# Modulation columns at fixed places, low parts of weights divided anew, a first norm that starts with TensorE, tiles 96 bytes further

## The chip, the cores and the metric

One core of a Trainium2 chip runs the whole program in one launch. The metric is the device time of that launch in microseconds (us). TensorE (PE in the profile) multiplies, VectorE (DVE) and ScalarE (ACT) work elementwise, GpSimd (POOL) does small elementwise work and issues some DMAs, and SyncE (SP) issues nearly all the others.

## The reference

A trunk of two layers over 512 frames of 1024 features, float32. Each layer has a token mixer and a SwiGLU network (MLP), both behind an RMS norm that a conditioning vector `c` scales and shifts:

```
mod = silu(c) @ ada_w[l] + ada_b[l]                     # 6 x 1024 columns: shift, scale, gate, twice
h   = rms_norm(x, norm1_g) * (1 + sc1) + sh1
p   = h @ w_in                                          # shifted features, pooled features, gates
ps  = token_shift(p[..., :N_SHIFT])                     # r, k, v, and three small "lora" inputs
y_a = rwkv7_time_mix(ps, ...)                           # a recurrence over the frames, 8 heads of 64
y_b = multiscale_pool(p[..., pooled part])
mixed = gate0 * (y_a @ proj_a) + gate1 * (y_b @ proj_b)
x   = x + gt1 * (mixed @ w_out)
h2  = rms_norm(x, norm2_g) * (1 + sc2) + sh2
x   = x + gt2 * ((silu(h2 @ w_gate) * (h2 @ w_up)) @ w_down)
...
return rms_norm(x, final_g)
```

## The kernel before

**Layout of the work.** Everything is transposed: a tile holds 128 features by 512 frames. A product of float32 accuracy is made of three fast passes: a weight tile `raw` of 128 x 1024 is split into a rounded high part `whi` and the rest `wlo`, the features likewise into `hh` and `hl`, and `block` (L224) issues `whi*hh`, `whi*hl`, `wlo*hh`. A stretch of such passes is called a block here; eight of them make one output tile.

**Low parts.** `weights` (L180) always lets ScalarE round `raw` into `whi`. The low part is made in one of two ways, chosen by `self.by_dma`: VectorE subtracts (`wlo<-raw,whi`, L201), or ScalarE writes `-whi` and a DMA on POOL's queue reads the weight a second time and adds it (L198 and L199). `by_dma = 2` alternates.

**Modulation.** One column of `mod` is a 128 x 1024 row block of `ada` multiplied by the broadcast `silu(c)` (`cact`) and summed, one VectorE instruction (L264, shown as CUSTOM_DVE_ANT_0) and a short read of its sum. `some` (L266) fetches the next row block and multiplies the one fetched before; `self.land` names the buffers for it (spare tiles `ar`, `hf`, `row`), else it lands in a `raw` buffer. There are 96 columns. Sixteen are made in the head, columns 16 to 47 of layer 0 in the first mixer, and the 48 of layer 1 in the first MLP and the second mixer. Where an instruction is not marked to keep its place (`self.exact`, L236), the scheduler chooses where it stands on its engine.

**Stages.** The head (`head`, L294) loads `c` (broadcast to 128 partitions) and `x`, sums squares (`ssum`), forms the reciprocal root (`rstd`, L403) by way of TensorE, and multiplies the first seven groups of columns of `w_in`, whose inputs `nh`, `hh`, `hl` become ready feature group by feature group (k = 0 to 7); for k below 3 the raw weights are used in plain float32. Then for each layer: `loras` and `pooled` (small products and running means), a loop over four head pairs j in which `front` and `back` prepare the recurrence on VectorE, ScalarE and POOL while `SLOT` says how many blocks of the next products run and where `some` is called; `solve` (a triangular inverse, 62 short VectorE instructions in a chain) with 51 blocks of gate products beside it; `chain`, the recurrence over eight chunks, in which TensorE's order is fixed (`pinned`): per chunk the products `z`, `u`, `hp`, `y`, with 1, 2 and 1 blocks of gate products between them (`CHAIN`); the read-out (`read`) with its copies `yn`, `yal`; `proj_a`; `w_out`; the second norm; and the MLP (`mlp`, L1351), in which 22 groups of hidden features, 19 of them by a scheme of seven products (`seven`), are followed by `w_down`.

In one chunk of the recurrence VectorE must deliver, in this order, `zs` (from `z`, needed by `u`), `vt` (from `u`, needed by `hp` and `y`), `hn` and the next `vt` (needed by the next `z`).

## Time and profile before

| | |
|---|---|
| median of 3 runs | 1476.82 us (1475.88 to 1486.47) |
| the profiled execution | 1479.65 us |
| its span, first to last instruction | 1477.9 us |
| mean granted TensorE clock | 0.995 |
| busy: PE, DVE, ACT, POOL | 97%, 74%, 51%, 17% |
| HBM read, written | 269.84 MB, 27.79 MB |

By time from the span's start: head 0 to 62 us, first mixer to 420, first MLP to 757, second mixer to 1125, second MLP and the end to 1478. A row of the timeline gives start, duration, engine, line, operation, output and inputs, and in brackets how long the engine was idle before it and what ended the wait. A row of waits gives the waiting engine and line, what it waited for, the total in us, how often, and the longest. A row of the windows gives, for a stretch of time, each engine's busy time with its count of instructions, the granted clock (1.00 is full), the DMA engines' busy share and GB/s.

### The profile page before, as it was taken

The page shows a single profiled execution, that of the slowest core. Times are in us where ns is not written, and L with a number is a line of the kernel's source. Part 1 is how long each engine was busy: PE and PEld are TensorE (multiplying, and loading weights), DVE is VectorE, ACT ScalarE, POOL GpSimd, SP SyncE. Part 2 cuts the span into 40 slices and gives each one's busy share as a digit, 9 for nine tenths or more (in the row PEclk, how much of TensorE's full clock was granted, in tenths as well). Part 3 has the DMA queues.
Part 4 walks back from the last instruction along what each step waited for, and adds up shares of the span by engine and source line. Part 5 has one row for each costly group of instructions (what it writes and reads, how often), then busy time and mean ns, then how long its engine had stood idle before and what let it go on. Part 6 is the DMA issues. An engine that isn't in the chain of part 4 may idle for free. (4 is left out here: it accounts for less than half of the span.)

```text
span 1477.9 us, 25375 instructions
## 1 busy us (share of the span) xinstructions
PE 1429.7 (97%) x9982; PEld 1219.6 (83%) x9982; DVE 1087.3 (74%) x1846; ACT 751.0 (51%) x1031; POOL 246.8 (17%) x291
## 2 busy tenths in 40 slices
PE   5999998999999999999999999999999999999998
PEld 2767676777899999988897777877789999998887
DVE  7888958576788888876767685768578888887333
ACT  5576544344456656642336766443444656656221
POOL 0133321110022211100012334111102222110000
PEclk9999999999999999999999999999999999999999
DMA  8788689589839999778726747976974899885232
GB/s 319 235 268 238 193 227 254 148 261 271 236 101 230 234 215 226 179 251 287 260 87 180 181 113 168 261 176 191 289 235 131 208 219 223 192 187 169 87 100 71
DMA packets 112918, 299.28 MB, mean 203 GB/s; under 512 B 12128, under 2 KB 22624, under 8 KB 112800
## 3 DMA queue, kind: packets, MB, share of 16 engines
q1 hardware_dynamic: 90160, 227.93, 47.3%
q0 software_dynamic: 21776, 68.69, 25.5%
q8 instruction: 78, 1.28, 0.4%
q10 hardware_dynamic: 864, 1.05, 0.2%
q14 instruction: 40, 0.33, 0.1%
HBM read 269.84 MB, written 27.79 MB: 201 GB/s over the span
## 5 line engine op out<-in xcount | busy, mean ns | idle before, releaser
L221 PE MATMUL acc<-hh,whi 128*128 128x512 f32 (+1 forms) x1119 | 392.5, 357 | 0.2
L221 PE MATMUL acc<-hh,wlo 128*128 128x512 f32 (+1 forms) x1111 | 379.2, 346 | 8.3 <-DMA wlo<-in_w_in 7.5
L221 PE MATMUL acc<-hl,whi 128*128 128x512 f32 (+2 forms) x1119 | 369.3, 346 | 0.1
L195 ACT CAST whi<-raw 128x1024 fp32r<-128x1024 f32 x143 | 149.8, 1049 | 266.8 <-PE acc L221 175.2
L221 PEld LDWEIGHTS acc<-hh,wlo 128*128 128x128 f32 x1111 | 210.7, 190 | 36.7 <-DMA wlo<-in_w_in 9.2
L221 PEld LDWEIGHTS acc<-hh,whi 128*128 128x128 f32 x1119 | 212.1, 190 | 31.9 <-issue 2.4
L221 PEld LDWEIGHTS acc<-hl,whi 128*128 128x128 f32 (+1 forms) x1119 | 203.8, 189 | 26.4 <-issue 2.2
L201 DVE TENSOR_TENSOR wlo<-raw,whi 128x1024 fp32r<-128x1024 f32 x78 | 94.7, 1221 | 77.3 <-ACT whi L195 72.9
L221 PE MATMUL acc<-f,whi 128*128 128x512 f32 (+1 forms) x304 | 92.2, 386 | 0.0
L221 PE MATMUL m<-tl,f13h 128*128 128x256 f32 x304 | 86.0, 283 | 0.0
L221 PE MATMUL m<-th,f13l 128*128 128x256 f32 x304 | 86.0, 283 | 0.0
L221 PE MATMUL m<-th,f13h 128*128 128x256 f32 x304 | 85.9, 283 | 0.0
L241 ACT CAST f24h<-x 128x1024 fp32r<-128x1024 f32 x38 | 39.9, 1050 | 60.4 <-DVE x L241 60.4
L198 ACT ACTIVATE wlo<-raw 128x1024 fp32r<-128x1024 f32 x65 | 68.5, 1053 | 0.1
L221 PEld LDWEIGHTS acc<-f,whi 128*128 128x128 f32 x304 | 56.2, 188 | 12.3
L199 POOL DMA_DIRECT2D wlo<-in_w_in x41 | 35.9, 876 | 159.3 <-ACT wlo L198 159.3
L1283 POOL DMA_DIRECT2D f22l<-in_w_gu x38 | 32.8, 863 | 171.6 <-ACT f22l L241 164.4
L221 PE MATMUL acc<-f,wlo 128*128 128x512 f32 (+1 forms) x152 | 58.7, 386 | 0.0
L241 DVE TENSOR_TENSOR f24l<-x,f24h 128x1024 fp32r<-128x1024 f32 x38 | 46.5, 1224 | 16.3 <-ACT f24h L241 16.3
L221 PEld LDWEIGHTS m<-th,f13h 128*128 128x128 f32 x304 | 58.4, 192 | 0.0
L221 PEld LDWEIGHTS m<-th,f13l 128*128 128x128 f32 x304 | 58.4, 192 | 0.0
L221 PEld LDWEIGHTS m<-tl,f13h 128*128 128x128 f32 x304 | 58.2, 192 | 0.0
(338 smaller groups left out, 3434.0 us busy)
## 6 DMA issues: line engine op xcount, KB each, us to landing
raw<-in_w_in SPq DMA_DIRECT2D x63, 512.0 KB, 4.7
raw<-in_w_gu SPq DMA_DIRECT2D x50, 512.0 KB, 4.5
raw<-in_w_down SPq DMA_DIRECT2D x44, 512.0 KB, 3.5
wlo<-in_w_in POOLq DMA_DIRECT2D x41, 512.0 KB, 7.7
wlo<-in_w_gu POOLq DMA_DIRECT2D x40, 512.0 KB, 6.8
x<-in_w_gu SPq DMA_DIRECT2D x76, 256.0 KB, 4.4
row<-in_ada SPq DMA_DIRECT2D x30, 512.0 KB, 5.2
raw<-in_ada SPq DMA_DIRECT2D x25, 512.0 KB, 4.9
```

Source lines behind the costliest of these rows:

```text
L195: self.on(nc.scalar, "copy")(hi, raw)
L198: nc.scalar.activation(lo, raw, AF.Copy, scale=-1.0)
L199: nc.gpsimd.dma_start(lo, src, accum_op=ALU.add)
L201: self.on(nc.vector, "tensor_tensor")(lo, raw, hi.bitcast(F32), ALU.subtract)
L221: i = (tensor.transpose if transpose else tensor.matmul)(*args, **k).ins
L241: return (lambda *a, **k: self.tc.keep_in_program_order(op(*a, **k))) if self.exact else op
L1283: nc.gpsimd.dma_start(lo, two[:, b], accum_op=ALU.add)
```

## The change

- **Head.** `c` comes as one row of 4 KB instead of a broadcast of 512 KB; two products with a row of ones spread it to 128 partitions, and ScalarE applies silu out of PSUM. TensorE runs 12, 14, 5 and 5 products of ones by ones (`idle`), whose results nobody reads, ahead of and between the steps of the norm. The first two modulation columns are made at fixed places, two of the four scalings `dg` go to ScalarE, and the squares have four buffers instead of two.
- **Columns.** None among the pooled groups (`SOME` 0 instead of 1), three instead of four per head pair at other places, five left for `w_out`, and in the first mixer one each at steps 2, 8, 14 and 20 of the recurrence (`LATER`), all of these marked to keep their place. Columns 40 to 47 of layer 0 move into the first MLP, where twelve instead of eight of its groups make one.
- **Low parts.** `by_dma` alternates for j = 0 and 4 in the first mixer and for j = 2, 3, 4 in the second, where it alternated for 2 and 3; from the end of the recurrence VectorE subtracts them all. In the whole program 112 low parts are subtracted on VectorE instead of 84, 28 fewer by DMA.
- **Order of blocks.** In the second mixer nine instead of three blocks of r, k, v run ahead of `loras`, with two weights loaded ahead, `loras` lands its inputs in halves in other buffers, and gate blocks follow when r, k, v are through.
- **Layout.** A pad of 88 float32 ahead of the left pools and one of 120 at the right edge. In the built program before, the starting addresses of the tiles that TensorE reads are 96, 160 or 224 past a multiple of 256 bytes (a few 64), and of the pairs of a moving tile and the next weights about half differ by 128, 64 or 192 modulo 256 in the 512-wide products; with the pads nearly all start at a multiple of 256, and all but some 70 pairs differ by 0.

```diff
+PADS = (88, 120)
-SOME = 1
+SOME = 0
+
+LATER = (2, 8, 14, 20)
+WARM = (12, 14, 5)
-FIRST = (8, 3)
+FIRST = (8, 9)
-        (0, False, 0), (3, True, 0), (3, False, 1), (2, False, 0), (4, True, 1), (3, False, 0), (3, False, 1),
-        (4, True, 1), (1, False, 0), (1, False, 0),
+        (0, False, 0), (3, True, 0), (3, False, 1), (2, False, 0), (4, True, 0), (3, False, 0), (3, False, 0),
+        (4, True, 1), (1, False, 0), (1, False, 1),
...
+        self.const.tile([P, PADS[0]], F32, name="pad")
+        pool(name="edge", bufs=1, side="right").tile([P, PADS[1]], F32, name="edge")
...
-        nc.sync.dma_start(self.cact, a["c"].partition_broadcast(P))
+        c = w0.tile([1, D], F32, name="c", bufs=1)
...
+        self.pinned = True
+        ps = [self.m() for _ in range(3)]
+        idle = lambda n: [self.mm(ps[2][:, 0:P], self.ones, self.ones, start=True, stop=True) for _ in range(n)]
+        idle(WARM[0])
+
+        def spread(i):
+            cs = slice(i * S, i * S + S)
+            self.mm(ps[i], self.ones[0:1, :], c[:, cs], start=True, stop=True)
+            nc.scalar.activation(self.cact[:, cs], ps[i], AF.Silu)
...
+            if k in (4, 5):
+                spread(k - 4)
+        idle(WARM[1])
         self.soon(AF.Sqrt)
+        self.exact = True
+        self.modulation(0, (KC,), raws)
         self.new_h()
-        rb = self.rstd(ALL)
+        rb = self.rstd(ALL, lambda: idle(WARM[2]))
+        idle(WARM[2])
+        self.modulation(0, (0,), raws)
+        self.exact = self.pinned = False
...
-            nc.vector.tensor_scalar(
-                dg[:, w * P : (w + 1) * P], self.c("ident"), r[:, w : w + 1], None, ALU.mult
-            )
+            o = dg[:, w * P : (w + 1) * P]
+            if n == 4 and w % 2:
+                self.on(nc.scalar, "activation")(o, self.c("ident"), AF.Copy, scale=r[:, w : w + 1])
+            else:
+                self.on(nc.vector, "tensor_scalar")(o, self.c("ident"), r[:, w : w + 1], None, ALU.mult)
...
-        self.ahead = 2 - l
+        self.ahead = 2
...
+            work = itertools.chain(st, gates)
...
-                self.by_dma = 2 if j in (2, 3) else True
+                self.by_dma = 2 if j in ((0, 4), (2, 3, 4))[l] else True
...
-                fill = st if j < NJ - 1 else gates
                 for n, ahead, some in SLOT[min(j, 1)]:
                     next(steps[ahead], None)
-                    self.go(fill, n)
+                    self.go(work, n)
                     if some:
+                        self.exact = True
                         self.some(1)
+                        self.exact = False
...
-                for step in self.chain(l, sc):
+                if l == 0:
+                    self.land = [gp.tile([P, D], F32, name="row")]
+                for n, step in enumerate(self.chain(l, sc)):
                     self.go(gates, CHAIN[step])
+                    if l == 0 and n in LATER:
+                        self.exact = True
+                        self.some(1)
+                        self.exact = False
+                self.flush()
+                self.land = []
             self.pinned = False
+            self.by_dma = False
...
-        self.some(len(self.todo) - 8)
+        self.some(len(self.todo) - 5)
...
-                        if (i + l) % (2 + l) == 0 and i < FC - 3:
+                        if (i % 3 == 2 if l else i % 4 < 3) and i < FC - 3:
                             self.some(1)
...
-        self.todo = [(0, i) for i in range(16, 48)]
+        self.todo = [(0, i) for i in range(16, 40)]
...
-                    self.todo += [(l + 1, i) for i in range(48)]
+                    self.todo += [(l, i) for i in range(40, 48)] + [(l + 1, i) for i in range(48)]
```

Three places show what this does to the order of instructions. The first is TensorE at the program's start, before, where the four means of `ssum` are its first products, `dg` spreads the reciprocal root, and `nh,wr` is the first block:

```order
L221 MATMUL m<-mean,ssum 128x1 x4
L221 MATMUL m<-dg,ones 128x512
L221 MATMUL acc<-nh,wr_147 128x512
L221 MATMUL acc<-nh,wr_148 128x512
L221 MATMUL acc<-nh,wr_150 128x512
```

The same place with the change:

```order
L229 MATMUL m<-ones 128x128 x12
L229 MATMUL m<-c,ones 128x512 x2
L229 MATMUL m<-ones 128x128 x14
L229 MATMUL m<-mean,ssum 128x1 x4
L229 MATMUL m<-ones 128x128 x5
L229 MATMUL m<-dg,ones 128x512
L229 MATMUL m<-ones 128x128 x5
L229 MATMUL acc<-nh,wr_173 128x512
```

TensorE has 36 products of ones and the two that spread `c` ahead of the first block.

The second is VectorE in the first mixer, in the preparation of a head pair by `front`, which ends in the product `sig<-r,cols,k` that TensorE's sum `m<-sig,cst` reads (`ar<-m,cst` is the mask of the pair before). Before (ISA is the instruction of one column):

```order
L264 ISA ar,mods_77<-ar,cact,cols 128x1024
L264 ISA mods_77 128x1
L754 RECIPROCAL n<-n 128x512
L603 SCALAR_TENSOR_TENSOR k<-acc,cols,k 128x511
L746 SCALAR_TENSOR_TENSOR lc<-cst,sig 128x512
L813 TENSOR_TENSOR ar<-m,cst 128x512
L750 TENSOR_SCALAR sig<-a,cols,omka_83 128x512
L813 TENSOR_TENSOR ar<-m,cst 128x512
L762 SCALAR_TENSOR_TENSOR n<-k,cols,n 128x512
L264 ISA ar,mods_77<-ar,cact,cols 128x1024
L264 ISA mods_77 128x1
L765 TENSOR_TENSOR k<-k,sig 128x512
```

(The update of `r`, L603, and the product `sig<-r,cols,k`, L772, follow.) With the change:

```order
L794 TENSOR_SCALAR n<-n 128x512
L795 RECIPROCAL n<-n 128x512
L639 SCALAR_TENSOR_TENSOR k<-acc,cols,k 128x511
L787 SCALAR_TENSOR_TENSOR lc<-cst,sig 128x512
L854 TENSOR_TENSOR ar<-m,cst 128x512
L791 TENSOR_SCALAR sig<-a,cols,omka_83 128x512
L854 TENSOR_TENSOR ar<-m,cst 128x512
L803 SCALAR_TENSOR_TENSOR n<-k,cols,n 128x512
L806 TENSOR_TENSOR k<-k,sig 128x512
L639 SCALAR_TENSOR_TENSOR r<-acc,cols,r 128x511
L813 SCALAR_TENSOR_TENSOR sig<-r,cols,k 128x512
```

No column stands ahead of the reciprocal or between `n` and `sig` any more; the three of this head pair stand behind the four products `bk` that follow `sig`.

The third is VectorE in the recurrence, third chunk, before, between the two halves of `yn` (the read-out of the chunks before):

```order
L961 TENSOR_TENSOR vt<-hn,pc 64x4x64
L1004 RECIPROCAL mv<-mv 128x8
L961 TENSOR_TENSOR vt<-hn,pc 64x4x64
L1010 TENSOR_SCALAR yn<-acc,mv 128x64 x4
L936 TENSOR_SCALAR zs<-m 128x256
```

With the change:

```order
L1002 TENSOR_TENSOR vt<-hn,pc 64x4x64
L1045 RECIPROCAL mv<-mv 128x8
L1002 TENSOR_TENSOR vt<-hn,pc 64x4x64
L1051 TENSOR_SCALAR yn<-acc,mv 128x64 x4
L249 ISA row,mods_77<-row,cact,cols 128x1024
L249 ISA mods_77 128x1
L977 TENSOR_SCALAR zs<-m 128x256
```

A column now stands directly ahead of `zs`, here and in the chunks of steps 14 and 20; the column of step 2 stands ahead of `zs` of the second chunk, with no `yn` there yet.

More of the change, by code (lines that the diff above doesn't have):

```diff
@@ L298, in head, with rows @@
         self.cact = self.const.tile([P, D], F32, name="cact")
-        nc.sync.dma_start(self.cact, a["c"].partition_broadcast(P))
         xin = [w0.tile([P, S], F32, name=f"xi{k}", bufs=1) for k in range(KC)]
+        c = w0.tile([1, D], F32, name="c", bufs=1)
+        raws, ws = {}, []
+        def rows(k, which=(KC, 0)):
+            for i in which:
+                raws[i + k] = self.rows(0, i + k, w0)
+        at = CST["block"][0]
         for k in range(KC):
             nc.sync.dma_start(xin[k], a["x"][k])
-        at = CST["block"][0]
-        nc.sync.dma_start(self.cst[:, 0:at], a["cst"][:, 0:at])
-        nc.sync.dma_start(self.cols, a["cols"])
+            if k == 1:
+                nc.sync.dma_start(c, a["c"].rearrange("(p n) -> p n", p=1))
+            if k == 3:
+                nc.sync.dma_start(self.cst[:, 0:at], a["cst"][:, 0:at])
+                nc.sync.dma_start(self.cols, a["cols"])
+        rows(0)
         nc.gpsimd.memset(self.ones, 1.0)
@@ L309, in head @@
         nc.gpsimd.memset(self.eps[:, 1:2], EPS_GN)
-        nc.scalar.activation(self.cact, self.cact, AF.Silu)
-        raws, ws = {}, []
-        def rows(k):
-            for i in (KC + k, k):
-                raws[i] = self.rows(0, i, w0)
+        self.soon(AF.Silu)
+        self.pinned = True
[6 more added lines that the diff above has]
+            nc.scalar.activation(self.cact[:, cs], ps[i], AF.Silu)
         raw = [w0.tile([P, D], F32, name=f"wr{i}", bufs=1) for i in range(KRV0)]
         cut = WHOLE * P
-        rows(0)
         for i in range(KRV0):
@@ L327, in head @@
             nc.sync.dma_start(raw[i][:, at:], a["w_in"][0, i][:, at:])
+        self.ssum = w0.tile([P, S], F32, name="ssum", bufs=1)
         for k in range(KC):
-            self.square(xin[k], k, ALL)
+            sq = w0.tile([P, S], F32, tag="sq", name="sq", bufs=4) if k else self.ssum
+            nc.scalar.activation(sq, xin[k], AF.Square)
+            if k:
+                nc.vector.tensor_tensor(self.ssum, self.ssum, sq, ALU.add)
+            if k in (4, 5):
+                spread(k - 4)
+        idle(WARM[1])
         self.soon(AF.Sqrt)
+        self.exact = True
+        self.modulation(0, (KC,), raws)
         self.new_h()
-        rb = self.rstd(ALL)
+        rb = self.rstd(ALL, lambda: idle(WARM[2]))
+        idle(WARM[2])
+        self.modulation(0, (0,), raws)
+        self.exact = self.pinned = False
         self.soon(AF.Sigmoid)
@@ L612, in loras @@
         sub = lambda out, x, hi: nc.vector.tensor_tensor(out, x, hi.bitcast(F32), ALU.subtract)
-        raw = [self.wraw.tile([P, 1024], F32, tag="raw", name="raw") for _ in range(3)]
-        nc.sync.dma_start(raw[0], self.a["wa_up"][l])
-        nc.sync.dma_start(raw[1][0:96, :], self.a["gv_up"][l])
-        nc.sync.dma_start(raw[2][:, 0:512], self.a["g_up"][l])
+        half = lambda i: slice(512 * i, 512 * i + 512)
+        if l:
+            raw = [self.pt("raw") for _ in range(5)]
+        else:
+            raw = [self.wraw.tile([P, 1024], F32, tag="raw", name="raw") for _ in range(3)]
+            raw = [t[:, half(i)] for t in raw for i in range(2)][:5]
+        for i in range(2):
+            nc.sync.dma_start(raw[i], self.a["wa_up"][l][:, half(i)])
+        for i in range(l + 1):
+            nc.sync.dma_start(raw[2 + i][0:96, :], self.a["gv_up"][l][:, half(i)])
+        nc.sync.dma_start(raw[-1], self.a["g_up"][l])
         self.wa = [sl.tile([P, n], F32R, name=f"wa{n}") for n in (1024, 512)]
-        nc.scalar.copy(self.wa[0], raw[0])
         for par, h, o in PARS:
-            cs = slice(par * 512, (par + 1) * 512)
-            sub(self.wa[1][h], raw[0][h, cs], self.wa[0][h, cs])
+            nc.scalar.copy(self.wa[0][:, half(par)], raw[par])
+            sub(self.wa[1][h], raw[par][h], self.wa[0][h, half(par)])
         self.wgv = [p.tile([96, 512], F32R, name="wgv") for p in (sm, sl)[: l + 1]]
         for i in range(l + 1):
-            cs = slice(512 * i, 512 * i + 512)
-            nc.scalar.copy(self.wgv[i], raw[1][0:96, cs])
-            sub(self.wgv[i][64:96], raw[1][64:96, cs], self.wgv[i][64:96])
+            nc.scalar.copy(self.wgv[i], raw[2 + i][0:96, :])
+            sub(self.wgv[i][64:96], raw[2 + i][64:96, :], self.wgv[i][64:96])
         self.wg = [sm.tile([P, 512], F32R, name=f"wg{i}") for i in range(2)]
-        self.split(*self.wg, raw[2][:, 0:512])
+        self.split(*self.wg, raw[-1])
         self.xwa = [sl.tile([P, S], F32R, name=f"xwa{i}") for i in range(2)]
```

9 lines of the change are left out of this document (5 added, 4 removed).

## Prediction

> **What bounds the kernel now.** The page comes first, for the engine that is always busy.
>
> ```profile
> span 1477.9 us, 25375 instructions
> PE 1429.7 (97%) x9982; PEld 1219.6 (83%) x9982; DVE 1087.3 (74%) x1846; ACT 751.0 (51%) x1031; POOL 246.8 (17%) x291
> ```
>
> TensorE is busy for 1429.7 of 1477.9 us, so only its 48 us of idle time and the pace of its products can give anything. The waits of TensorE say where the idle time lies: by stretch, first the first mixer up to the recurrence (60 to 260 us), then the second (780 to 960) and from its solve to its norm (960 to 1125).
>
> ```profile
> PE m L221 <- POOL omka L383: 13.2, 1, 13.2
> ...
> PE acc L221 <- DMA wlo<-in_w_in: 6.0, 3, 3.1
> PE m L221 <- DVE sig L772: 4.4, 2, 3.6
> PE m L221 <- DVE pd L703: 1.5, 2, 1.3
> PE m L221 <- DVE xgv L612: 0.5, 1, 0.5
> ...
> PE m L221 <- ACT whi L195: 1.7, 1, 1.7
> PE acc L221 <- DMA wlo<-in_w_in: 1.5, 1, 1.5
> ...
> PE acc L221 <- DMA wlo<-in_proj_a: 1.0, 1, 1.0
> PE acc L221 <- DMA wlo<-in_w_out: 0.5, 1, 0.5
> ```
>
> The first row is the head, 13.2 us before TensorE has anything to do (the engine named is only the last of several). The first mixer waits 12.4 us in these rows, the second 4.7. Last, the windows:
>
> ```profile
> 160.00:180.00 20.00, 17.35 (x83) 12.15 (x84) 17.87 (x23) 11.87 (x14) 6.40 (x7) 0.83 0.63 183
> 220.00:240.00 20.00, 16.87 (x69) 13.41 (x68) 18.26 (x50) 7.40 (x9) 2.58 (x3) 0.91 0.96 259
> 480.00:500.00 20.00, 20.00 (x170) 20.00 (x169) 16.99 (x27) 12.16 (x17) 4.58 (x6) 1.00 0.94 240
> ```
>
> In the MLP (480 to 500) TensorE never waits. In the first mixer two waits cost twice: the granted clock falls to 0.83 and 0.91 in their windows.
>
> **The head.** Its chain, in the timeline:
>
> ```profile
> 7.55 5.47 DVE L402 TENSOR_TENSOR ssum<-ssum,sq 128x512 f32<-128x512 f32 x7 [7.55 <-ACT sq L401]
> 13.17 1.84 PE L221 MATMUL m<-mean,ssum 128*128 128x1 f32 x8 [13.17 <-POOL omka L383]
> 15.56 0.88 DVE L417 TENSOR_SCALAR dg<-cst,r 128x128 f32<-128x128 f32 x4
> 16.35 1.28 DVE L264 CUSTOM_DVE_ANT_0 raw<-raw,cact,cols 128x1024 f32<-128x1024 f32 x1
> 16.58 2.04 PE L221 MATMUL m<-dg,ones 128*128 128x512 f32 x2 [1.57 <-DVE dg L417]
> 18.66 1.28 DVE L354 TENSOR_TENSOR nt<-xi,m 128x512 f32<-128x512 f32 x2 [1.03 <-PE m L221]
> 20.25 4.60 PE L221 MATMUL acc<-nh,wr 128*128 128x512 f32 x6 [1.63 <-ACT nh L356]
> ...
> 27.27 2.74 PE L221 MATMUL acc<-nh,wr 128*128 128x512 f32 x6
> 0.00:20.00 20.00, 3.88 (x10) 2.28 (x10) 9.62 (x19) 10.90 (x16) 2.17 (x12) 1.00 0.94 335
> ```
>
> The seven sums end at 13.02, and every later step hangs on them. The broadcast of `c`, 512 KB ahead of `x`, takes 1.5 us at this window's 335 GB/s; without it the sums end about 1.5 us earlier. The first products run at half clock, though the window's clock column says 1.00: six `nh,wr` take 4.60 us from 20.25 and six later ones 2.74. With the idle products ahead, 1.84 and 2.04 us halve: 0.9 and 1.0. The four `dg` on two engines give 0.4. The column at 16.35 now starts with `dg`'s end and outlasts the faster product by 0.3. So `nt` comes 1.5 + 0.9 + 1.0 + 0.4 - 0.3 = 3.5 us earlier. The first block would gain 1.9 us more by the full clock, but not the stage:
>
> ```profile
> 38.05 0.62 ACT L245 CAST hh<-nh 128x512 fp32r<-128x512 f32 x1
> 38.74 1.10 PE L221 MATMUL acc<-hh,whi 128*128 128x512 f32 x4
> ```
>
> Group k = 3 is ready at 38.67 and TensorE takes it at 38.74; VectorE has worked without a pause since `nt`. So I take -3.5 us, between -1.5 (the DMA alone) and -5.4 (VectorE catches up). The 36 idle products cost nothing while the sums and `dg` are what TensorE waits for.
>
> **The first mixer, up to the recurrence.** VectorE's own waits from 60 to 215 us, and what stood behind one of them:
>
> ```profile
> DVE raw L264 <- DMA raw<-in_ada: 14.1, 3, 7.2
> DVE ar L264 <- DMA ar<-in_ada: 8.1, 4, 3.6
> ...
> 148.99 1.29 DVE L264 CUSTOM_DVE_ANT_0 ar<-ar,cact,cols 128x1024 f32<-128x1024 f32 x1 [3.65 <-DMA ar<-in_ada]
> 150.21 3.35 DVE L754 RECIPROCAL n<-n 128x512 f32<-128x512 f32 x1
> 161.50 1.00 DVE L772 SCALAR_TENSOR_TENSOR sig<-r,cols,k 128x512 f32<-128x512 f32 x1
> 162.65 2.05 PE L221 MATMUL m<-sig,cst 128*128 128x512 f32 x2 [3.57 <-DVE sig L772]
> ```
>
> VectorE lost 22.2 us to columns whose rows had not landed, with the reciprocal and `sig` queued behind; TensorE waited 3.57 us for `sig` and then ran at half clock until 167.2. The change takes 8 of 23 columns out of this stretch (8 x 1.36 us, instruction and read) and puts the rest behind `sig`, one use after their fetch. I count both waits for `sig` as gone: 4.4, and half of the 4.5 us of slow clock, 2.3. From the waits for `pd` and `xgv` (2.0), where four columns went, I take half: 1.0.
>
> By the Trainium skill (TensorE: Matmul & The Clock Gate, Part 1) a whole window of about 3.4 us without work halves the clock; the trace agrees for the 3.57 us gap, but a gap of 3.13 us did it too. By that rule the short gaps that I expect below would not slow the clock.
>
> ```profile
> 225.66 0.79 PE L221 MATMUL acc<-hh,wlo 128*128 128x512 f32 x1 [3.13 <-DMA wlo<-in_w_in]
> wlo<-in_w_in POOLq DMA_DIRECT2D x41, 512.0 KB, 7.7
> L201 DVE TENSOR_TENSOR wlo<-raw,whi 128x1024 fp32r<-128x1024 f32 x78 | 94.7, 1221 | 77.3 <-ACT whi L195 72.9
> ```
>
> A low part by DMA takes 7.7 us to land, 1.22 us on VectorE. From POOL's order, 13 low parts by DMA stand ahead of the solve and 7 between it and the recurrence before; now 12 and 3. Of the 6.0 us of waits and 1.5 us of slow clock after 225.66 I take 5.5. Together -13.2 us, between -5 (only `sig`, less what other columns delay) and -16.
>
> The Trainium skill (SBUF — State Buffer, on the port pair that VectorE and GpSimd share) lets a VectorE instruction with two SBUF inputs lock out a GpSimd one that reads SBUF, which speaks against subtracting beside POOL's work; no wait of the first mixer's TensorE names POOL, so I charge nothing for it.
>
> **The recurrence.** Here the change adds work to an engine that others wait for:
>
> ```profile
> 282.39 1.10 DVE L1010 TENSOR_SCALAR yn<-acc,mv 128x64 f32<-128x64 f32 x4
> 283.58 0.43 DVE L936 TENSOR_SCALAR zs<-m 128x256 f32<-128x256 f32 x1
> 284.36 0.68 PE L221 MATMUL m<-zs,tt 64*64 64x64 f32 x16
> 300.00:320.00 20.00, 19.94 (x244) 15.00 (x243) 17.12 (x65) 8.65 (x12) 3.86 (x5) 1.00 0.96 259
> ```
>
> In a chunk TensorE needs `zs` for its next product: `zs` ends at 284.01 and the sixteen products `zs,tt` start at 284.36, 0.35 later. A column takes 1.36 us. Three of the four stand directly between `yn` and `zs`: `zs` would run 284.94 to 285.37, `zs,tt` could start at 285.72, and only the products that now stand behind it from 285.07 cannot be brought forward, since the order is fixed. So TensorE stands up to 1.36 us; of the waits ahead of `vt` it may win back some, and I take 1.0 each, 3.0. The first column has no `yn` ahead of it: 0. Of low parts, each layer gets 1 between the first and last `zs` and 3 in the last read-out, 1.22 us each on VectorE in place of a DMA: 8 in all, of which I count 4 us, since the read-out's own chain (`yn`) is VectorE's. Together +7.0, between 0 and +15.2 (4 x 1.36 + 8 x 1.22 in full). VectorE is at 17.12 of 20 us here, so the 68 us from 262 to 330 have some 10 us free and the first layer's part of that is 5.4 + 4.9: just what it holds.
>
> **The second mixer.** Its waits are the last four rows of the first list. The one for `whi` (1.7, ahead of `loras`) and the first for `wlo` (1.5) are covered by nine blocks instead of three or by two weights loaded ahead: half of each. Those for `wlo` of `proj_a` (1.0) and of `w_out` (0.5) are for low parts by DMA that VectorE now subtracts: gone. -3.1 us, between 0 (VectorE is as late) and -4.7.
>
> **Layout.** Two windows, cut at starts of products, in which TensorE never waits and only 512-wide products run, 42 and 48 of them:
>
> ```profile
> 659.79:669.57 9.78, 9.78 (x43) 7.88 (x42) 8.83 (x14) 2.74 (x3) 0.00 (x0) 1.00 0.85 289
> 426.98:437.88 10.90, 10.90 (x50) 9.01 (x49) 9.07 (x11) 6.30 (x12) 2.08 (x3) 1.00 0.34 102
> ```
>
> By the addresses of the built program, moving tile and next weights start 128 bytes apart modulo 256 in the first, 0 apart in the second: 9.78 / 42 = 232.9 ns a product against 10.90 / 48 = 227.1. Over the whole trace the mean distance of starts is 228.1 ns at 0 apart, 229.3 at 64, 232.8 at 128 and 233.3 at 192 for 512-wide pairs (3119 in all, 1173 of them at 128, 238 at 64, 105 at 192), so all at 0 save 1173 x 4.7 + 238 x 1.2 + 105 x 5.2 = 6.3 us. For 256-wide ones it is 119.8 at 0, 118.7 at 128 (1225) and 116.9 at 192 (378): 2.4 us lost. -4.0 us. No tile of before starts at a multiple of 256, so what that does in itself no row shows. Bounds: if it slows the pairs that are at 0 now to the slow class, 1603 x 4.7 = +7.5; if it gains as much once more as the two windows differ (5.8 ns on 3119), -4.0 - 18.1 = -22. I take the row that exists, with no effect of its own.
>
> **Columns in the MLP.** Eight more columns go to the first MLP, and four more of its groups make one. The window 480 to 500 holds two groups of `seven` (10.0 us each) and VectorE has 16.99 of 20 with one column in one of the two; a group with a column then has 9.2 of 10.0. Hidden: 0, and up to 8 x 1.36 = 10.9 us only if VectorE were full. The 28 DMAs less (14.7 MB, some 29 us of ScalarE's time at 1053 ns each) free engines that nobody waits for.
>
> **The sum.** -3.5 - 13.2 + 7.0 - 3.1 - 4.0 = -16.8 us. The profiled execution took 1479.65 us (span 1477.9), so 1462.9 by it; it lies 2.8 above the median of the runs, so on that the forecast is 1476.8 - 16.8 = 1460.0 us.
>
> **Rivals.** Forecast (0.58): 1460, own range 1450 to 1468.
>
> Layout quickens every product (0.12): the absolute start counts as much as the distance did, -18.1 more: 1441.9. For it: the 5.8 ns that one pair's position is worth. Against: the 64-apart class hardly differs from 0, so it's a matter of the pair.
>
> The recurrence takes it back (0.15): all columns and low parts there in full, +15.2 instead of +7.0: 1468.2. For it: VectorE's spare 10 us are spent exactly. Against: only three of the columns stand directly ahead of something TensorE needs.
>
> Columns and low parts wait as before (0.09): the fixed places meet rows that land as late as now (a column fetched one use ahead), so that the first mixer gives 5 and the second nothing: -3.5 - 5 + 7 - 4 = -5.5, 1471.3. For it: rows of `ada` took up to 7.2 us longer than their use. Against: then `bk` waits, not `sig`.
>
> VectorE becomes the bound of both mixers (0.06, the slower side): some 14 low parts from the solves to the read-outs (4 and about 3 in each layer, 17.1 us) and four columns (5.4) are all in front of what TensorE needs, and the columns behind `sig` keep the pairs from gaining anything: +22.5 - 3.5 = +19, 1495.8. It decides once VectorE's share of the recurrence, 86% now, reaches 100%, which is 10 us of added work in one layer.
>
> **Chances and range.** About 1%, 14.8 us, is what a measurement of this kernel can tell from no change: faster is below 1462.0, slower above 1491.6. The forecast lies 2 us beyond the bound, so two thirds of it count as faster (0.39), with the layout case (0.12) and a little of the others (0.03): 0.54. Slower 0.05, the last rival but for its lower edge; the rest, 0.41, within 1%. The range reaches from 1438 (layout case, less the 4 that the head or the mixers may add) to 1477 (the two milder rivals and no change); outside lie the last rival and some tails.
>
> **What would show it.** Right: `nt` starts near 15.2 instead of 18.66 and the first `nh,wr` already run at the later pace; no wait of VectorE for rows of `ada` with a reciprocal behind it, and no 3 us wait of TensorE for `sig` or for `wlo` beside the solve; in layer 0's third, fifth and seventh chunk a wait of TensorE for `zs` of about 1 us; no DMA waits in `proj_a`; products of `w_down` at 227 ns. Wrong: `zs` or `vt` waits in every chunk (VectorE is the bound), MLP groups longer than 10.0 us with TensorE waiting for VectorE, a clock below 1.00 at a new place, or `w_down` at a pace outside 227 to 233 ns.

## The result and the profile after

The changed kernel takes 1461.11 us (median of 6 runs, 1460.17 to 1463.69) against 1476.35 us for the kernel before (6 runs beside it): a ratio of 0.9892 with a 95% interval of 0.9865 to 0.9918. The forecast was 1460.0. The profiled execution took 1461.8 us with a span of 1460.0, so 17.9 us of span are gone where 16.8 were forecast; by the medians it is 15.2, since the profiled execution of the kernel before lies 3.3 above its median here. The first lines of its page:

```profile
span 1460.0 us, 25496 instructions
PE 1434.3 (98%) x10058; PEld 1236.2 (85%) x10058; DVE 1112.6 (76%) x1872; ACT 722.9 (50%) x1008; POOL 220.6 (15%) x263
```

TensorE's idle time fell from 48.2 to 25.7 us (span less busy; the 36 idle products count as busy). To see where, I take the starts of the first product of each stage from both timelines, and give the length of each stage in us, one execution of each kernel:

| stage (layer) | before | after | difference | forecast |
|---|---|---|---|---|
| head, up to the first block | 20.2 | 17.6 | -2.7 | -3.5 |
| first mixer, up to the recurrence | 245.4 | 231.1 | -14.3 | -13.2 |
| recurrence (0), first to last chunk's `zs,tt` | 46.4 | 50.3 | +3.9 | together with the read-outs +7.0 |
| read-out, proj_a, w_out (0) | 88.2 | 82.8 | -5.4 | |
| second norm, MLP (0) | 416.6 | 417.6 | +1.0 | -0.9 for `whi`; layout -4.0, all stages |
| second mixer, up to the recurrence | 164.0 | 164.7 | +0.7 | -0.7 |
| recurrence (1) | 46.3 | 52.4 | +6.1 | (above) |
| read-out, proj_a, w_out (1) | 89.3 | 83.2 | -6.1 | -1.5 |
| second norm, MLP (1), end | 355.4 | 354.3 | -1.0 | |

About 4.1 us of blocks moved in layer 1 from the row "read-out" to the row "MLP (0)" (six blocks more run ahead of the small products), so these two rows are -2.0 and -3.1 when the same work is compared ("at equal work" below). The sum agrees with the forecast and so do its first two terms. The layer 1 recurrence doesn't: the change puts no column there.

The head first, in the timeline:

```profile
12.51 1.02 PE L229 MATMUL m<-mean,ssum 128*128 128x1 f32 x8 [0.24 <-DVE ssum L354]
14.83 1.13 PE L229 MATMUL m<-dg,ones 128*128 128x512 f32 x2
15.99 1.28 DVE L388 TENSOR_TENSOR nt<-xi,m 128x512 f32<-128x512 f32 x2 [0.23 <-PE m L229]
17.58 2.84 PE L229 MATMUL acc<-nh,wr 128*128 128x512 f32 x6 [0.51 <-ACT nh L390]
```

The two small steps run at full clock (1.84 to 1.02, 2.04 to 1.13) and the first block too (4.60 to 2.84). The means start 0.66 us earlier, at 12.51, where 1.5 was forecast for the smaller load of `c`; `nt` starts at 15.99, forecast 15.2.

The waits of TensorE, by stretch: the first mixer up to the recurrence (60 to 250 us), the recurrence of layer 0 (248 to 300), the second mixer (765 to 963), and the recurrence of layer 1 with its read-out and proj_a (963 to 1060):

```profile
PE m L229 <- DVE tn L921: 2.7, 2, 1.7
PE m L229 <- DVE xgv L648: 0.6, 1, 0.6
...
PE m L229 <- DVE zs L977: 1.6, 3, 0.8
PE m L229 <- DVE vt L1002: 0.6, 1, 0.6
...
PE acc L229 <- DVE wlo L209: 2.2, 1, 2.2
PE m L229 <- DVE sig L838: 0.9, 1, 0.9
...
PE m L229 <- DVE vt L1002: 3.5, 1, 3.5
PE acc L229 <- DVE hl L569: 1.5, 1, 1.5
```

The first mixer's waits for `sig` (4.4) and for low parts by DMA (6.0) are gone, as forecast; a wait for `tn`, the end of the solve's chain on VectorE, is new. VectorE waits for rows of `ada` there for 4.1 us instead of 22.2. The three waits for `zs` in the recurrence of layer 0 stand behind the columns, in its fourth, sixth and eighth chunk. In the second mixer the wait of 1.5 us for a low part by DMA is gone, and one of 2.2 us for a low part that VectorE makes has come. The wait of 3.5 us for `vt` in layer 1 is new, and no step of the prediction expects it. The timeline at that place:

```profile
997.40 0.69 DVE L569 TENSOR_TENSOR hh<-acc,g 128x512 f32<-128x512 f32 x1 [3.68 <-DMA g<-gd]
998.13 0.42 DVE L1002 TENSOR_TENSOR vt<-hn,pc 64x256 f32<-64x256 f32 x1
998.61 1.12 PE L229 MATMUL m<-vt,ar 128*64 128x64 f32 x14 [3.49 <-DVE vt L1002]
984.00:1004.00 20.00, 16.51 (x193) 12.40 (x192) 13.01 (x47) 8.50 (x12) 2.12 (x3) 0.83 0.60 172
```

`hh<-acc,g` (`side`, the proj_b stage) multiplies a finished block by a gate tile that was stored in DRAM and is read back. The tile had not landed; VectorE stood for 3.68 us, `vt` behind it, and TensorE for 3.49 us behind that. The window's granted clock is 0.83, and the trace has TensorE at half clock from 997.4 to 1004.2: the stall costs twice, as `sig` did before. The Trainium skill (TensorE: Matmul & The Clock Gate, section "Architectural detail: the array is 16× 32×32, not 1× 128×128") calls VectorE's queue strictly first in, first out; the trace agrees, `vt` starts 0.73 us after the product that stood ahead of it.

Layout, in the window of the same 42 products of `w_down` as before:

```profile
641.44:650.96 9.52, 9.52 (x43) 7.89 (x42) 8.77 (x14) 2.74 (x3) 0.00 (x0) 1.00 0.84 271
```

9.52 / 42 = 226.7 ns against 232.9 before: what was forecast (227).

### The profile page after: what moved, and what is told of

Read it like the earlier page. It is cut to its first block, busy times and chain, and to the rows that moved or that the text cites. A ratio compares the mean times of both kernels' runs of the same rounds, so it can differ in the third digit from the quotient of the medians.

```text
span 1460.0 us, 25496 instructions
## 1 busy us (share of the span) xinstructions
PE 1434.3 (98%) x10058; PEld 1236.2 (85%) x10058; DVE 1112.6 (76%) x1872; ACT 722.9 (50%) x1008; POOL 220.6 (15%) x263
## 3 DMA queue, kind: packets, MB, share of 16 engines
q10 hardware_dynamic: 864, 1.05, 0.2%
## 4 chain that ended last, share of the span: by engine, by line
PE 87%; DVE 6%; DMA 3%; ACT 2%; issue 1%; SPq 0%; POOL 0%; DVEq 0%; ACTq 0%
PE acc L229 63%; PE m L229 24%; DVE wlo L209 1%; DMA g<-gd 1%; DVE raw L272 1%; ACT whi L203 1%; DMA d<-vf 1%; DMA wlo<-in_w_in 1%; DMA raw<-in_w_in 0%; DVE tmp L909 0%; DVE T L915 0%; DMA xi<-in_x 0%; DVE tn L921 0%; DVE yn L1051 0%; ACT nh L390 0%
## 5 line engine op out<-in xcount | busy, mean ns | idle before, releaser
L209 DVE TENSOR_TENSOR wlo<-raw,whi 128x1024 fp32r<-128x1024 f32 x106 | 129.9, 1229 | 90.6 <-ACT whi L203 90.2
L249 DVE TENSOR_TENSOR f24l<-x,f24h 128x1024 fp32r<-128x1024 f32 x38 | 46.5, 1224 | 14.2 <-ACT f24h L249 14.2
L249 ACT ACTIVATE s<-s 128x512 f32<-128x512 f32 x38 | 24.0, 632 | 65.0 <-DVE s L249 65.0
L249 DVE TENSOR_TENSOR x<-raw,x 128x512 f32<-128x512 f32 x76 | 52.4, 689 | 1.3
```

The costliest lines, as they stand in the source:

```text
L209: self.on(nc.vector, "tensor_tensor")(lo, raw, hi.bitcast(F32), ALU.subtract)
L249: return (lambda *a, **k: self.tc.keep_in_program_order(op(*a, **k))) if self.exact else op
```

## The experiments

Each kernel was timed against the kernel before on its chip. The time is a median; the ratio is to the kernel before, with its 95% interval. Differences in us between two kernels are of medians from different chips, whose kernel before has medians of 1476.4 to 1478.0 us; where that matters, the ratios are compared too. Stage lengths are worked out as in the table above, from one execution of each kernel.

**1. Gate tiles of their own in layer 1.** The stall of layer 1 by itself:

```diff
-                self.stream(items[:-2]), self.abreast(items[-2:]), self.side(l, gate, lambda n: fresh(n))
+                self.stream(items[:-2]), self.abreast(items[-2:]), self.side(l, gate, lambda n: fresh("own" if l else n))
```

> The changed kernel, where in layer 1 the gate tiles that the proj_b stage loads in the recurrence get two buffers of their own instead of those that the last gate products still write, so that the first load can be issued early. TensorE's order is the same. Theory: TensorE's 3.5 us wait for vt in the fourth chunk of layer 1, and about 1.5 us of halved clock behind it, come from vt standing behind a product with a gate tile that has not landed; both go, -5 us, about 1456. Rival: vt is late for another reason there (VectorE is simply behind by its added low parts): the wait stays over 2 us and the time within 1 us of 1461.

1457.99 us, ratio 0.9863 (0.9842 to 0.9883): 3.1 us under the changed kernel in the medians, 4.3 by the ratios, 7.6 in the profiled executions. The two intervals overlap, so the whole time alone doesn't settle it; the stages do. The recurrence of layer 1 falls from 52.4 to 46.1 us (46.3 before the change), proj_a from 24.4 to 22.4. The waits from 955 to 1045 us no longer hold `vt`:

```profile
PE acc L229 <- ACT yah L1069: 1.5, 1, 1.5
PE m L229 <- DVE zs L977: 0.5, 1, 0.5
```

With TensorE's order unchanged, the late tile is shown to be the cause. In the changed kernel the two buffers `g` are written by the last gate products (stored at 987.8 to 989.1 us), and the first load is issued behind them, at 990.0, for a product that runs at 997.4. With buffers of its own it is issued at 917.4 and has landed at 922.8.

**2. Order of blocks as before.** The two weights loaded ahead and the loads of `loras` stay as changed.

```diff
-FIRST = (8, 9)
+FIRST = (8, 3)
...
-            work = itertools.chain(st, gates)
...
+                fill = st if j < NJ - 1 else gates
...
-                    self.go(work, n)
+                    self.go(fill, n)
```

> The changed kernel with the order of blocks as before: three blocks of r, k, v ahead of the small products in layer 1, gate blocks only from the last head pair on. Theory (the gate blocks that run earlier bring the proj_b stage earlier into the recurrence of layer 1, where its first gate tile has not landed): the 3.5 us wait for vt in layer 1 goes, -5 to -7 us there; the waits for whi and wlo ahead of the second mixer's small products return, +2 to +3: 1457 to 1459. Rival (the wait comes from the fewer low parts by DMA or from VectorE's place for the product, not from the order): the wait for vt stays, 1463 or more.

1460.88 us, ratio 0.9897 (0.9877 to 0.9918): no different from the changed kernel. The theory's mechanism holds: no wait of TensorE is left from 960 to 1060 us, and the recurrence of layer 1 takes 46.8 us. But the price of the old order was set too low. The second mixer up to its recurrence takes 170.7 instead of 164.7 us, with waits for `tn` (3.3) and `wlo` by DMA (2.6) that were not there:

```profile
PE m L229 <- DVE tn L921: 3.3, 2, 1.7
PE acc L229 <- DMA wlo<-in_w_in: 2.6, 1, 2.6
```

So, with the rest as changed, the new order wins 9.3 us at equal work ahead of the recurrence of layer 1 (5.9 in the second mixer, 3.4 in the stage before it) and loses 10.1 in it and up to the norm (5.6 and 4.5). That is no gain on the kernel before: its second mixer, with the old order and the old division of low parts, takes 164.0 us and has no wait for `tn`. In these traces the new order makes up for what the rest of the change costs in that stage, and no more.

**3. No columns in the recurrence.** The four are made in w_out:

```diff
-LATER = (2, 8, 14, 20)
+LATER = ()
...
-        self.some(len(self.todo) - 5)
+        self.some(len(self.todo) - (9, 5)[l])
...
-                self.some(1)
+                self.some(1 + (l == 0 and m < 4))
```

> The changed kernel without columns in the recurrence of layer 0; the four are made in w_out, whose five steps make nine columns instead of five. Theory (three columns delay zs by 1 us each): the recurrence of layer 0 gets some 2.5 to 3 us shorter, w_out hides the columns, 1458. Rival A (low parts and not columns take the time there): within 1 us of 1461, the waits for zs stay. Rival B (w_out cannot hide four more): slower than 1461, with waits for rows of ada or for modulation ahead of the second norm.

1460.16 us, ratio 0.9882 (0.9863 to 0.9902): within what the medians can tell of the changed kernel. The stages tell more: the recurrence of layer 0 falls from 50.3 to 46.5 us, where it was 46.4 before, and w_out stays at 42.0. No wait of TensorE for `zs` is left there. So columns and not low parts hold the recurrence up, by 3.8 us (forecast 3.0 for columns). 1.8 us more are spent ahead of the recurrence in this execution, in the head, the loop of head pairs and the solve, where nothing was changed; experiment 1, which leaves layer 0 alone, has 1.6 us more there too.

**4. All columns as before,** with the rest changed: `SOME`, `SLOT`, the free places, eight in w_out, the lists `todo`, the MLP's rate.

```diff
-SOME = 0
+SOME = 1
...
-LATER = (2, 8, 14, 20)
+LATER = ()
...
-        self.todo = [(0, i) for i in range(16, 40)]
+        self.todo = [(0, i) for i in range(16, 48)]
```

> The changed kernel with the modulation columns as before: one per pooled group, four per head pair at the old places and free to move, eight in w_out, none in the recurrence, 40 to 47 of layer 0 not in the MLP. Theory (the first mixer's gain of 14 us came half from columns): TensorE's 3 to 4 us waits for sig with halved clock behind them return, 7 to 9 us up to the recurrence, less 3.8 us that the recurrence wins: 1465 to 1467. Rival A (columns were harmless, the low parts and the order of blocks gave the first mixer's gain): 1457, the 3.8 us alone. Rival B (columns gave all of it): 1470 or more.

1480.44 us, ratio 1.0017 (1.0003 to 1.0031): 19.3 us slower, rival B. The first mixer takes 256.9 us instead of 231.1. TensorE's and then VectorE's waits there (60 to 260, 60 to 235 us), and three windows:

```profile
PE m L229 <- DVE sig L813: 7.3, 2, 4.6
PE acc L229 <- DMA wlo<-in_w_in: 3.7, 1, 3.7
...
DVE ar L272 <- DMA ar<-in_ada: 14.7, 6, 6.5
DVE raw L272 <- DMA raw<-in_ada: 9.6, 3, 4.8
140.00:160.00 20.00, 17.52 (x110) 13.11 (x109) 12.08 (x16) 8.42 (x11) 4.32 (x6) 0.97 0.84 241
160.00:180.00 20.00, 17.28 (x83) 11.60 (x85) 16.10 (x23) 14.68 (x20) 7.57 (x6) 0.78 0.71 173
180.00:200.00 20.00, 15.04 (x93) 10.88 (x92) 16.74 (x19) 10.63 (x14) 7.08 (x7) 0.83 0.72 219
```

The picture of the kernel before, only worse: VectorE waits 24.3 us for rows, `sig` is late behind them, and the clock is 0.78 and 0.83 over 40 us.

**5. Low parts divided as before.**

```diff
-                self.by_dma = 2 if j in ((0, 4), (2, 3, 4))[l] else True
+                self.by_dma = 2 if j in (2, 3) else True
...
-            self.by_dma = False
```

> The changed kernel with the low parts divided as before: by DMA and VectorE in turn for j = 2 and 3 in both mixers, by DMA elsewhere, in recurrence, read-out and proj_a too. Theory: the wait for a low part by DMA beside the solve and in the loop of head pairs returns (the 5.5 us of the prediction), the waits in proj_a and w_out too (1.5 or more), while the solve of layer 0 wins its 2.7 us of waits for tn and the recurrences little (under 1 us): 1464 to 1468. Rival (low parts on VectorE cost in the recurrence what the prediction charged, 4 us, and DMA would have been in time): 1457 to 1461.

1481.70 us, ratio 1.0032 (1.0014 to 1.0051): 20.6 us slower, outside both expectations. Up to the recurrence it is 2.2 us faster than the changed kernel (228.9 against 231.1 us), so VectorE's low parts gain nothing there: the loop of head pairs is 1.2 us longer without them, and the solve 3.4 shorter. The loss comes later: 56.3 instead of 50.3 us in the recurrence of layer 0, 90.5 instead of 82.8 from its read-out to the norm, and some 5 us in layer 1. The timeline of the recurrence of layer 0 has the stall of experiment 1:

```profile
294.01 0.69 DVE L569 TENSOR_TENSOR hh<-acc,g 128x512 f32<-128x512 f32 x1 [5.37 <-DMA g<-gd]
295.08 1.51 PE L229 MATMUL m<-vt,bt 128*64 128x64 f32 x16 [4.66 <-DVE vt L985]
```

The load for this product is issued earlier than in the changed kernel, at 284.4 instead of 287.3 us, and lands later, 9.5 us after its issue instead of 4.7. In the 20 us around it the queue of the low parts by DMA moves 1.05 MB instead of 0.52.

**6. The same, with gate tiles of their own** (every other one in layer 0, where room is short):

```diff
-                self.stream(items[:-2]), self.abreast(items[-2:]), self.side(l, gate, lambda n: fresh(n))
+                self.stream(items[:-2]), self.abreast(items[-2:]), self.side(l, gate, lambda n: fresh("own") if l else own(n))
...
+            turns = itertools.count()
+            own = lambda n: fresh(n) if next(turns) % 2 else gp.tile([P, S], F32, tag="own", name="own", bufs=1)
```

> The kernel with the low parts divided as before, and gate tiles of the proj_b stage in buffers of their own (every other one in layer 0, all in layer 1), everything else as changed. Theory: low parts by DMA cost time in the recurrence not by themselves but because a gate tile, issued late from a shared buffer into a busy DMA, lands late and stands on VectorE ahead of vt. Then TensorE's waits for vt of 4.7 us (layer 0) and 3.3 us (layer 1) go, with the slow clock behind them: -8 to -13 us against the old division alone, some 1470. Rival (the low parts' own landing is what is late): the waits stay or turn into waits for wlo, 1478 or more.

1467.62 us (1458.57 to 1474.71), ratio 0.9937 (0.9916 to 0.9958): 14.1 us better than experiment 5, and no wait of TensorE for VectorE's `vt` is left. The recurrences take 49.7 and 46.1 us instead of 56.3 and 52.4. Some of this is the late tile of layer 1, which the changed kernel has too. Against experiment 1, which has the same tiles of its own in layer 1, the old division costs 9.6 us instead of 20.6. So about half of its cost is the late gate tile; the rest shows as waits for `wlo` by DMA (2.7), for `mh` (2.3) and for `yn` (2.2), of which the changed kernel has 0.3 in all.

**7. Both as before,** experiments 4 and 5 together.

> The changed kernel with both the columns and the division of low parts as before, so that of the change only head, order of blocks and layout are left. Undoing columns alone cost 19 us and undoing the low parts alone 21 us. If the two work by separate stalls, 1461 + 19 + 21 = 1501. If they are worth something only together (columns at fixed places need rows that land in time, which the DMA freed by VectorE's low parts gives, and VectorE's low parts need the room that the moved columns leave), 1468 to 1478: about the kernel before, less the head and the layout.

1480.23 us, ratio 1.0026 (1.0010 to 1.0041). The two don't add: of 1501 there is nothing. It is also above the 1468 to 1478 of the other expectation: what is left of the change, head, order of blocks and layout, gains nothing on the kernel before (1476.5 on that chip) when the two parts are missing.

| | low parts as before | divided anew |
|---|---|---|
| columns as before | 1480.2 | 1480.4 |
| columns at fixed places | 1481.7 | 1461.1 |

Either alone does nothing, both together take 19 us away. By stages, from the profiled executions (that of "neither" took 1489.5 us, 9.3 above its median, with the excess in layer 1):

| us | neither | low parts only | columns only | both |
|---|---|---|---|---|
| first mixer, to the recurrence | 246.5 | 256.9 | 228.9 | 231.1 |
| recurrence (0) | 46.3 | 46.5 | 56.3 | 50.3 |
| read-out to norm (0) | 87.5 | 82.8 | 90.5 | 82.8 |

The columns give the first mixer 18 to 26 us. The division costs 10 us there as long as columns stand in VectorE's way, and 2 without them; its gain lies in the recurrence, only when columns are in it, and behind it.

**8. Addresses 128 bytes apart again.** Only the right-hand pad differs:

```diff
-PADS = (88, 120)
+PADS = (88, 152)
```

> The changed kernel with the right-hand pad 32 float32 (128 bytes) longer and nothing else, so that 1152 of the 512-wide and 1225 of the 256-wide pairs of moving tile and next weights start 128 bytes apart modulo 256 again, as in the kernel before. Theory (the distance within a pair sets the pace): 1152 x 4.7 ns - 1225 x 1.1 ns = +4.1 us, about 1465, the second half of the w_down products back near 233 ns, everything else as in the changed kernel. Rival (the absolute start at a multiple of 256 bytes is what counts): half of the tiles lose it, so 256-wide products slow down as well and the loss is 8 us or more. Second rival (addresses do nothing): 1461.

1465.74 us, ratio 0.9916 (0.9899 to 0.9932): +4.6 us by the medians, +3.5 by the ratios, theory +4.1; the interval overlaps that of the changed kernel (0.9865 to 0.9918). The 42 products of `w_down` are back:

```profile
643.33:653.12 9.79, 9.79 (x43) 7.88 (x42) 8.83 (x14) 2.74 (x3) 0.00 (x0) 1.00 0.84 271
```

9.79 / 42 = 233.1 ns. All 462 products of `w_down` take 1.8 and 2.0 us longer in the two layers. The 256-wide products of the MLPs' seven-product groups get 0.9 and 0.7 us shorter, as the class means of before have it (118.7 ns at 128 apart, 119.8 at 0). So 2.2 us are seen directly in the MLPs; the rest of the profiled difference lies in the mixers, where waits differ too (last section).

**9. No pads.**

```diff
-        self.const.tile([P, PADS[0]], F32, name="pad")
-        pool(name="edge", bufs=1, side="right").tile([P, PADS[1]], F32, name="edge")
```

> The changed kernel without the two pads. Its tiles start at 160 and 224 modulo 256, its pairs are 0, 64 or 192 apart, hardly any 128. Theory (distance within a pair, with the class means of the trace before: 228.1, 229.3, 233.3 ns at 0, 64, 192 for 512-wide pairs, 119.8 and 116.9 at 0 and 192 for 256-wide ones): the sum comes out the same as with the pads, within 1 us, so 1461. Rival (the absolute start counts): slower by 5 us or more, near 1466 to 1475.

1462.35 us, ratio 0.9898 (0.9881 to 0.9915): +1.2 us, no clear difference. The 42 products take 229.3 ns each, the mean of pairs 64 apart before. Against the changed kernel `w_down` loses 1.3 us in each layer and the 256-wide products of the groups of seven win 1.6. So it is the distance within a pair that counts; that tiles start at a multiple of 256 bytes gives nothing that these runs can see. The pads by themselves are worth little, since the change's other tiles had already moved the pairs away from 128.

**10. No idle products in the head.**

```diff
-WARM = (12, 14, 5)
+WARM = (0, 0, 0)
```

> The changed kernel without the 36 idle products in the head. Theory: the means and the spread of the root run at half clock again, 0.8 and 0.9 us longer, so nt starts 1.7 us later, and the stage with it, 1463; the first six products of the first block take 4.6 instead of 2.84 us, which costs nothing, since VectorE's work on the groups sets the stage. Rival A (the slow first block counts too): 1464.7. Rival B (another part of the head, the smaller load of c, sets nt): 1461.

1459.86 us, ratio 0.9881 (0.9859 to 0.9903): no loss in the median. The head itself is 1.9 us longer (expected 1.7), and the small products of layer 0 start 1.3 us later. That isn't seen in the whole, because in this execution the gate tile of layer 1 landed earlier (recurrence 47.5 instead of 52.4 us). What the idle products gain is shown for the head, 1.3 us at its end, and not for the whole.

**11. Own gate tiles and no columns in the recurrence,** experiments 1 and 3 together.

> The changed kernel with the two edits together: own gate tiles in layer 1, and no columns in the recurrence of layer 0. If the two stalls are separate places on TensorE's path, their gains add: the recurrence of layer 0 falls from 50.3 to about 46.5 us, that of layer 1 from 52.4 to about 46.1, proj_a of layer 1 by 2, so -10 to -12 us by the profiles and, since the runs showed about half of that in the medians, -5 to -10 in the median: 1451 to 1456. Rival (what is won in the recurrence is lost behind it, in w_out or in the second mixer): 1458 or more.

1453.92 us, ratio 0.9844 (0.9822 to 0.9866): -7.2 us, and the recurrences take 46.5 and 46.2 us. In layer 0 the solve takes 18.6 us from its first `tn,ar` to the recurrence against 15.7, though nothing was changed there (17.1 in experiments 1, 8 and 10):

```profile
233.84 0.22 PE L229 MATMUL m<-tn,ar 32*32 32x32 f32 x2 [2.69 <-DVE tn L921]
235.74 1.68 PE L229 MATMUL m<-tn,ar 32*32 32x32 f32 x62 [1.69 <-DVE tn L921]
230.00:245.00 15.00, 10.62 (x150) 7.80 (x150) 13.12 (x13) 7.21 (x10) 0.86 (x1) 0.70 0.41 107
```

**12. The same, without VectorE's low parts beside the solve of layer 0.**

```diff
-                self.by_dma = 2 if j in ((0, 4), (2, 3, 4))[l] else True
+                self.by_dma = 2 if j in ((0,), (2, 3, 4))[l] else True
```

> The kernel with own gate tiles and no columns in the recurrence, and in layer 0 VectorE subtracts low parts in turn for j = 0 only, not for the last group beside the solve. Theory: the low part of 1.22 us inside the solve's chain on VectorE goes, and with it TensorE's waits for tn (4.4 us in that kernel, 2.7 in the changed one) and the slow clock behind: -3 to -5, 1449 to 1451. Rival (the low parts by DMA land too late there, as in the kernel before): a wait for wlo by DMA comes back, 1454 or more.

1450.92 us (1449.08 to 1453.83), ratio 0.9827 (0.9808 to 0.9847): the fastest of all, 10.2 us under the changed kernel, and the only one whose interval lies wholly below that of the changed kernel. The wait for `tn` is gone, that stretch takes 12.8 us, and its window is at full clock:

```profile
230.00:245.00 15.00, 14.76 (x297) 11.46 (x296) 13.05 (x9) 11.15 (x14) 0.86 (x1) 1.00 0.78 195
```

A wait for `wlo` by DMA of 2.4 us (two places) is the price.

## Why the prediction was right, and where only its sum was

The time is within 1.1 us of the forecast, and the stages bear out the total of the largest term, not its parts. Term by term:

- **Head, -3.5 against -2.7.** The halved small products were right (0.8 and 0.9). The mis-sized term is the load of `c`: the means start 0.66 us earlier and not 1.5, since the squares under the sums now wait for `x` (ScalarE for 1.4 and 0.7 us, none before).
- **First mixer, -13.2 against -14.3.** The named waits went, but the split was wrong, and that the total holds is luck. The columns alone give 17.6 us (246.5 to 228.9); the prediction had 7.7 for them. The new division of low parts, put at -5.5, costs 2.2 there: the wait for `wlo` beside the solve goes, and one for `tn` comes, because a subtraction stands inside the solve's chain (experiment 12). The prediction took a queue's relief for a gain without asking what the same work does on VectorE at that place.
- **Recurrence, +7.0.** Columns were right in size (3.0 against 3.8) and in place (the chunks that the prediction counts as third, fifth and seventh), but only 1.6 of it are waits for `zs`, 0.2 to 0.8 each where about 1 was expected; the rest are waits for `vt`, `yn` and `g` of 0.3 to 0.6. The 4 us for low parts have the wrong sign: in the changed kernel they save 6.0 us in the recurrence of layer 0 and 7.7 behind it against the old division. The prediction weighed VectorE's time, and not that a second reading of the weights lies in the way of the gate tiles (9.5 us to landing instead of 4.7 in experiment 5).
- **Second mixer, -3.1.** The waits at proj_a and w_out went (-2.0 at equal work), and the wait for `whi` ahead of `loras` (1.7 to 0.2). The wait of 1.5 for `wlo` didn't get shorter: one of 2.2 for VectorE's low part took its place. And the new order costs in the recurrence: the gate blocks end earlier, the proj_b stage begins earlier, and its gate tile isn't there (+6.1). This step of the prediction failed: it listed what the order covers and not which loads the order brings forward to a busy queue. The costliest new wait of the changed kernel was none of its rivals.
- **Layout, -4.0.** Right in mechanism: 226.7 ns forecast as 227, `w_down` is 2.0 us shorter in each layer, and undoing it costs 3.5 to 4.6 us, with intervals that overlap. The rival that absolute addresses quicken everything is refuted by experiment 9.
- **MLP columns, 0.** Right: the groups of seven take 191.5 us in both layers against 191.4 and 191.2, eight more columns in the first.

Two errors of 6.5 and 5.0 us cancelled, which is luck too. In layer 0 the recurrence with what follows up to the norm was forecast at +5.0 (3.0 for columns, half of the low parts) and gave 3.9 - 5.4 = -1.5. In layer 1 the second mixer with its recurrence and read-out was forecast at 2.0 - 0.7 - 1.5 = -0.2 (the wait for `whi` lies in the row before) and gave, at equal work, 0.7 + 6.1 - 2.0 = +4.8. The rival "the recurrence takes it back" had the place of the second and not its cause. One of the prediction's signs of being wrong did appear, a clock below 1.00 at new places: 0.89 at the solve and 0.83 in the recurrence of layer 1.

## What to carry to other kernels

When work moves to an earlier place, follow the loads that it needs: a load into a buffer that is still in use is issued late, and on a queue that serves in order the late operand stops whatever stands behind it, here the one short instruction that TensorE needs. Two edits that relieve one queue and load another should be tried together and apart: alone, each of the two main parts of this change was worth nothing, and so was the rest of it without them. A forecast by stages should be checked by stages, since the sum can be right with two terms wrong.

## What the runs showed that was not expected

The clock halves without a wait as long as the 3.13 and 3.57 us of before. In the changed kernel two short waits at the solve do it:

```profile
232.97 0.22 PE L229 MATMUL m<-tn,ar 32*32 32x32 f32 x2 [1.00 <-DVE tn L921]
234.87 1.19 PE L229 MATMUL m<-tn,ar 32*32 32x32 f32 x62 [1.68 <-DVE tn L921]
235.99 0.62 PE L229 MATMUL acc<-hh,whi 128*128 128x512 f32 x1
236.41 0.63 PE L229 MATMUL acc<-hl,whi 128*128 128x512 f32 x1
230.00:245.00 15.00, 12.31 (x251) 9.32 (x251) 14.08 (x12) 9.59 (x13) 0.85 (x1) 0.89 0.42 92
```

1.00 and 1.68 us, with 0.22 us of small products between, and the next products start 0.42 us apart instead of 0.23. The prediction's sentence by the Trainium skill (TensorE: Matmul & The Clock Gate, Part 1), that short gaps would not slow the clock since it takes a whole window of some 3.4 us without work, is not borne out here: 2.9 us that were nearly empty were enough, and the measurement decides.

The traces say more. Their records of the granted clock change in steps of 3.41 us, and cut into such windows the changed kernel shows what decides, at the solve, at VectorE's low part in the second mixer and at proj_a of layer 1, each with the window after it:

```profile
232.81:236.22 3.41, 1.57 (x65) 1.45 (x66) 3.35 (x3) 0.17 (x1) 0.56 (x1) 1.00 0.87 176
236.22:239.63 3.41, 3.41 (x42) 2.36 (x43) 3.38 (x3) 2.86 (x4) 0.00 (x0) 0.50 0.72 135
864.20:867.61 3.41, 1.82 (x8) 1.51 (x9) 2.86 (x4) 0.91 (x2) 2.44 (x2) 1.00 0.40 53
867.61:871.02 3.41, 3.41 (x17) 2.23 (x15) 0.69 (x2) 1.16 (x2) 0.00 (x0) 1.00 1.01 299
1031.53:1034.94 3.41, 1.35 (x6) 0.76 (x5) 2.42 (x3) 1.48 (x2) 0.00 (x0) 1.00 0.96 333
1034.94:1038.35 3.41, 3.41 (x8) 2.68 (x9) 0.00 (x0) 0.00 (x0) 0.00 (x0) 0.50 0.67 226
```

TensorE was busy for 1.57, 1.82 and 1.35 of 3.41 us; behind the first and the third the clock is 0.50, behind the second 1.00. Over the 14 traces (30 us from the start to 20 before the end) half clock follows all 36 windows at full clock in which TensorE was busy for less than half, 9 of 25 between 50% and 63%, and none of 5669 above. So here it is the idle share of a window that counts and not the length of one wait. The same wait can cost once and not the next time, by where a window ends: the 1.46 us for `yah` in layer 1 are followed by half clock in the trace of experiment 3 and by full clock in that of experiment 1 (TensorE busy for 53% and 55% of the window).

The wait of 2.2 us for VectorE's low part is 4.2 us long in the traces of experiments 5, 7, 8 and 9, and the second mixer takes 167.1 to 169.3 us there, against 163.7 to 165.5 in the others with the new order. The low part itself is stretched, with a product of POOL beside it; first in the changed kernel, then in experiment 8:

```profile
864.51 1.23 DVE L209 TENSOR_TENSOR wlo<-raw,whi 128x1024 fp32r<-128x1024 f32 x1
865.12 1.77 POOL L834 TENSOR_TENSOR d<-d,v 128x512 f32<-128x512 f32 x1
...
867.10 3.20 DVE L209 TENSOR_TENSOR wlo<-raw,whi 128x1024 fp32r<-128x1024 f32 x1
867.66 1.55 POOL L834 TENSOR_TENSOR d<-d,v 128x512 f32<-128x512 f32 x1
```

In the second case the low part takes 2.0 us longer and POOL's product 0.2 less. That POOL's product causes it is not shown, since no run moves it away; the prediction named the pair and charged nothing for it.
